# Ordering the square sums of a merge's weights behind the ACT work traced ahead of them

## The chip, the cores and the metric

The kernel runs on one core of one Trainium2 chip. The metric is the device time of one execution, in microseconds (us). TensorE is called PE here, VectorE DVE, ScalarE ACT, GpSimd POOL and SyncE SP; SP issues most of the DMA transfers.

## The reference

One layer of a flow-matching backbone, for 2048 sample tokens and 128 prompt tokens, with a model width of 1024 and three branches of width 512. Cut to what matters here:

```python
proj = einsum('btd,de->bte', xn, w_in)      # xn: RMSNorm with adaLN
o_a = rmsnorm(delta_bidir(q, k, v, g, beta, s0_f, s0_b)) * silu(z_a)
o_b = chunk_sgu(u_b, v_b, sgu_norm_g, w_spatial, b_spatial) * silu(z_b)
o_c = fourier_mix(x_c, grid) * silu(z_c)
br = stack([o_a, o_b, o_c], axis=2)
pb = einsum('btnw,nwd->btnd', br, w_branch)
gt = sigmoid(gates.reshape(B, T, 3, 1024))  # gates: 3072 columns of proj
merged = einsum('btnd,btnd->btd', gt, pb)
y = rmsnorm(h + gate * einsum('btd,de->bte', merged, w_out), final_g)
```

The delta rule of branch A is a scan over chunks of tokens, forward and backward, and each step needs the state that the last step left. All data are float32.

## The kernel before

**Numbers.** A float32 product is made from float16 parts: each operand is scaled by a power of two and split into a high part and a rest, and three matmuls (high by high, high by rest, rest by high) sum up in PSUM. `gemm_T` does that for one weight block of 128 output columns and one token tile: 24 matmuls where the sum runs over 1024, 12 where it runs over 512.

**Weights.** `wlist` holds 84 blocks of weights in the order of their use: 4 for the gate of branch A, 32 for the projections of the branches, then 48 for the merges, a gate block (128 columns of w_in, 1024 by 128) and a branch block (128 columns of w_branch, 512 by 128) in turn. A block is read into a tile `wst` by SP (`read_w`, L195; two buffers) and made ready by the generator `converting`, in three steps:

1. ACT squares the block and sums the squares into `ss` (L209; the squares themselves go into the `lo` tile and are scratch), and DVE rounds the sum to bfloat16 (L175).
2. A small matmul with ones adds up over the partitions, and DVE works out the power-of-two scale and its inverse (L183 to L187, L220).
3. ACT writes the high part `hi` (L222) and DVE the rest `lo` (L223). After that the `wst` buffer is free.

`weight_step` makes one step each time `pace.tick` is called, which is once a token tile; `getw(n, ahead)` hands out the next n blocks, completes them where they aren't ready, and lets `ahead` more be begun. `wnext[0]` counts the blocks handed out.

**Merges.** `merge` runs three times: for branch 1, then 2, then 0. Each time it goes over 8 blocks of 128 output columns, and in each block over five token tiles (four of 512 and one of 128; the first two merges begin with tokens 0 to 1023, the third with the rest). For a tile it traces the gate product (24 matmuls), ACT's sigmoid of it (`sg`, L1385), the branch product (12 matmuls), one DVE pass that multiplies the two (L1391 in the first merge, L1394 in the others), a POOL addition to the running sum `mrow` (L1395), and `pace.tick`. The conversion of a next gate block is begun at the first tick of a block, and that of a next branch block at the fourth. In the third merge each block begins with the conversion of a block of w_out as well (`out_w`, by `load_w`), which goes through the same `converting`.

**The delta scan beside it.** The scan of branch A is a generator that `pace` advances while the projections and the first two merges are traced: some of its steps come out after every second k step of a `gemm_T`. On ACT its work is many small passes: splits into high part and rest (L907), the scaled output (L917, L1051), copies of small blocks (L860 to L894). The scan has ended before the third merge begins.

**What sets the order.** The program is traced in the order of the code; each engine's queue is then ordered by a scheduler at compile time, with its own times for every instruction and transfer: an instruction may go ahead of others that were traced before it when, by these times, its inputs are there and its engine is free. `tc.high_priority()` (around the sigmoid and the scales) ranks work ahead. On the chip every engine takes its queue in order: an instruction that waits holds up all that stand behind it.

Of the kernel before, what the change touches and what calls it, by code (L numbers as in the profile page):

```python
# [14 lines left out]
AF = mybir.ActivationFunctionType  # L15
# [96 lines left out]
def hybrid_flow_kernel(ctx: ExitStack, tc: tile.TileContext, x_prompt, x_sample, state_delta, c, c_ctx, ln_g, w_ada,  # L112
                       b_ada, w_in, conv_w, a_log, dt_bias, o_norm_g, sgu_norm_g, w_spatial, b_spatial, w_branch,
                       w_out, final_g, consts, y_prompt, y_sample, new_state, dbg=None):
    nc = tc.nc
    V, A, G, PE, SY = nc.vector, nc.scalar, nc.gpsimd, nc.tensor, nc.sync
# [9 lines left out]
    def sb(pl, shape, tag, dt=F32, bufs=None):  # L126
        kw = {} if bufs is None else {"bufs": bufs}
        return pl.tile(list(shape), dt, tag=tag, name=nm(tag), **kw)
# [31 lines left out]
    def mm(out, l, r, start=True, stop=True):  # L160
        PE.matmul(out, l, r, start=start, stop=stop)  # L161

    def mm3(out, l, r):
# [2 lines left out]
        mm(out, l[0], r[1], False, False)  # L166
        mm(out, l[1], r[0], False, True)

    def rsqrt(out, ss, mul, w):
        V.tensor_scalar(out, ss, mul, EPS, ALU.mult, ALU.add)  # L170
        G.tensor_tensor(out, out, mhalf.to_broadcast([P, w]), ALU.pow)  # L171

    def widened(ss, pl, tag):
        sb16 = sb(pl, [P, 1], tag + "b", BF16)
        V.tensor_copy(sb16, ss)  # L175
        return sb16

    def scales(ss, pl, tag, sb16=None):

        ps = bank(ps_x, [P, 1])  # L180
        mm(ps, ones16, widened(ss, pl, tag) if sb16 is None else sb16)
        t = sb(pl, [P, 4], tag)
        V.tensor_copy(t[:, 0:1], ps)  # L183
        h = t[:, 3:4].bitcast(I32)
        V.tensor_scalar(h, t[:, 0:1].bitcast(I32), 24, None, ALU.logical_shift_right)
        V.tensor_scalar(t[:, 1:2].bitcast(I32), h, -8388608.0, 204.0 * 8388608, ALU.mult, ALU.add)
        V.tensor_scalar(t[:, 2:3].bitcast(I32), h, 8388608.0, 50.0 * 8388608, ALU.mult, ALU.add)  # L187
        return t[:, 1:2], t[:, 2:3]
# [9 lines left out]
    def converting(w, st, nkt, cols=P, hi=None, lo=None, tag="w", bufs=5):  # L198

        wpool = bwp[0] if tag == "b" else wp  # L200
        if tag == "z":
            hi, lo = [sb(p0p, [P, nkt, cols], n_, F16, bufs=4) for n_ in ("zhi", "zlo")]
        if tag == "v":
            hi, lo = [t[:, vfilled[0]] for t in v4]
            vfilled[0] += 1
        w.hi = sb(wpool, [P, nkt, cols], tag + "hi", F16, bufs=bufs) if hi is None else hi
        w.lo = sb(wpool, [P, nkt, cols], tag + "lo", F16, bufs=bufs) if lo is None else lo
        ss = sb(wp, [P, 1], "wss", bufs=4)
        A.activation(w.lo, st, AF.Square, accum_out=ss)  # L209
        yield  # L210
        sb16 = widened(ss, wp, "wsc")
        if wnext[0] < 11:
            yield
        if wnext[0] < 16:
            s, inv = scales(None, wp, "wsc", sb16)
        else:
            with tc.high_priority():
                s, inv = scales(None, wp, "wsc", sb16)
        w.inv = sb(wp, [P, 1], "winv", bufs=10)
        V.tensor_mul(w.inv, inv, isx)  # L220
        yield
        A.activation(w.hi, st, AF.Copy, scale=s)  # L222
        V.scalar_tensor_tensor(w.lo, st, s, w.hi, ALU.mult, ALU.subtract)  # L223

    def convert(st, nkt, *args, **kw):
        w = _W()
        for _ in converting(w, st, nkt, *args, **kw):
            pass
        return w
# [22 lines left out]
        return xs_[t0:t0 + n, :] if t0 < NS else xp_[t0 - NS:t0 - NS + n, :]  # L252

    wlist = []
    for c0 in [C_ZA + g * P for g in range(4)]:
        wlist.append((w_in_[:, c0:c0 + P], KT, "z", 4))
    for c0 in ([C_QKV + i * P for i in range(12)] + [C_V + g * P for g in range(4)]
# [8 lines left out]
    wdone, wnext, wread, wlate, bwp, wsteps = [], [0], [], [0], [], []  # L266
# [6 lines left out]
    def begin():  # L273

        i = len(wdone)
        if i >= goal[0] or (wlist[i][2] == "b" and not bwp):
            return False
        if len(wread) == i:
            read_next()
        wdone.append(_W())  # L280
        wsteps.append(converting(wdone[i], wread[i], wlist[i][1], tag=wlist[i][2], bufs=wlist[i][3]))
        return True
# [15 lines left out]
    def getw(n=1, ahead=0):  # L298
        i = wnext[0]
        wnext[0] += n  # L300
        fetch(i + n)
        while len(wdone) - len(wsteps) < i + n:
            weight_step()
        fetch(i + n + ahead)
        r = wdone[i:i + n]
        return r[0] if n == 1 else r
# [89 lines left out]
    for blk in range(8):  # L396
# [4 lines left out]
        for k0 in range(0, KT, 4):  # L401
            st = sb(p0p, [P, 4, 256], "ast", bufs=8)
# [39 lines left out]
    for ti, (t0, tn) in enumerate(TBS):  # L442
# [7 lines left out]
        for j in range(nt):  # L450
            A.activation(jk, xt[:, j, :], AF.Square, accum_out=xss[:, j:j + 1])
        rs = sb(p0p, [P, nt], "rs")
        rsqrt(rs, xss, 1.0 / D, nt)
        for j in range(nt):
            V.tensor_scalar(xt[:, j, :], xt[:, j, :], rs[:, j:j + 1], None, ALU.mult)
# [166 lines left out]
    for ct in range(12):  # L622
        w = getw(1, 2 if ct < 6 else min(4, 15 - ct))
# [418 lines left out]
    def finish(t, o):  # L1042
        of = sb(dq, [P, WB], "of")
        SY.dma_start(of, ofD[t])
        G.tensor_tensor(o, o, of, ALU.add)
        ss = sb(dq, [P, H], "oss")
        for h in range(H):
            A.activation(of[:, hs(h)], o[:, hs(h)], AF.Square, accum_out=ss[:, h:h + 1])
        rsqrt(ss, ss, 1.0 / P, H)
        for h in range(H):  # L1050
            A.activation(o[:, hs(h)], o[:, hs(h)], AF.Copy, scale=ss[:, h:h + 1])  # L1051
        yield 1
        ps = bank(ps_out, [P, WB])
        for h in range(H):
            PE.transpose(ps[:, hs(h)], o[:, hs(h)], ident)  # L1055
        SY.dma_start(h3(of), szD[:, :, t * P:(t + 1) * P].rearrange("h p t -> p h t"))
        V.scalar_tensor_tensor(o, ps, ong, of, ALU.mult, ALU.mult)
        A.activation(of, o, AF.Square, accum_out=oss[0][:, t:t + 1])
        SY.dma_start(obD[0][:, :, t * P:(t + 1) * P].rearrange("h p t -> p h t"), h3(o))
# [111 lines left out]
    for t in range(NCH):  # L1171
        ps = bank(ps_mm, [P, 4, P])
        ts = slice(t * P, (t + 1) * P)
        for k in range(KT):
            mm(ps, xh[:, k, ts], v4[0][:, :, k, :], k == 0, False)
            mm(ps, xh[:, k, ts], v4[1][:, :, k, :], False, False)
            mm(ps, xl[:, k, ts], v4[0][:, :, k, :], False, k == KT - 1)
        vn = sb(ep, [P, WB], "sg", bufs=4).rearrange("p (i c) -> p i c", i=4)
        with tc.high_priority():
            V.tensor_tensor(vn, ps, vinv.rearrange("p (i o) -> p i o", o=1).to_broadcast([P, 4, P]), ALU.mult)  # L1180
        sq = sb(ep, [P, WB], "st", bufs=3)
        ss = sb(bp, [P, 1], "vss", bufs=3)
        A.activation(sq, vn.rearrange("p i c -> p (i c)"), AF.Square, accum_out=ss)
        rsqrt(ss, ss, 1.0 / WB, 1)
        if vprev is not None:
            spatial(*vprev)
        if len(vout) > 2:
            vstore()
        V.tensor_scalar(vn, vn, ss, None, ALU.mult)
        vprev = (t, vn)  # L1190
        if t == 8:
            cfill = fourier_consts()
        if t >= 8:
            next(cfill, 0)
        pace.tick(5.2)
# [9 lines left out]
    for g in range(4):  # L1205
# [5 lines left out]
        for ti, (t0, tn) in enumerate(TBS):  # L1211
            st = vrow[:, t0:t0 + tn]
# [349 lines left out]
```

## Time and profile before

| | |
|---|---|
| Median of 3 runs | 2200.02 us (2197.28 to 2202.29) |
| The profiled execution's own time | 2200.34 us |
| Its span, first to last instruction | 2198.2 us |
| Granted PE clock, mean | 0.993 |
| PE busy | 2125.9 us, 97% of the span |
| ACT busy | 1014.4 us, 46% |
| First merge, about | 1050 to 1415 us |
| Second merge, about | 1415 to 1745 us |
| Third merge, about | 1745 to 2020 us |

In the lines of the profile, L161 is line 161 of the kernel; most matmuls have that line, because one helper issues them. `wlo<-wst` is an instruction that reads the tile wst and writes wlo (gate weights); `blo` is the branch weights' tile, `wolo` that of w_out. A group line gives a count (x6), the shortest, median and longest duration in ns, and the first and last start in us. A line in order of time gives the start and the duration in us, and in square brackets how long the engine stood idle before it and what ended the wait. A matmul's duration there is its passage through the array; the next one starts before it has ended.

### The profile page before, as it was taken

What the parts mean: (1) busy time and instruction counts of PE and PEld (TensorE: products, weight loads), DVE (VectorE), ACT (ScalarE), POOL (GpSimd) and SP (SyncE); (2) the same over time, 40 slices, a digit from 0 to 9 for tenths busy, and PEclk for the clock granted to TensorE, in tenths of its full rate; (3) what the DMA queues carried; (4) which work ended last, traced back from release to release, by engine and by line L of the source; (5) the groups of instructions that cost most, each with busy time, mean ns of one, the idle gap of its engine ahead of it and who ended that gap; (6) DMA issues with size and microseconds to landing.
All of it is one profiled execution on the core that took longest, in us unless ns stands there. A gap on an engine that the chain in (4) does not pass through costs nothing. (4 is left out here: it accounts for less than half of the span.)

```text
span 2198.2 us, 42667 instructions
## 1 busy us (share of the span) xinstructions
PE 2125.9 (97%) x16234; PEld 1213.1 (55%) x16234; DVE 1311.2 (60%) x3140; ACT 1014.4 (46%) x2345; POOL 707.5 (32%) x862
## 2 busy tenths in 40 slices
PE   7999999999999999899899999999999999999998
PEld 3565444455555587777555555555654444444443
DVE  5746745469979698466665555765674544223454
ACT  3644644345466474355544445655553422222332
POOL 1421433223333322432322223344532221222543
PEclk9999999999999999999999999999999999999999
DMA  8324733167777662444655556776664544324542
GB/s 280 141 87 149 260 117 110 61 203 231 241 229 239 198 192 83 126 130 137 203 172 162 164 164 185 240 212 209 200 198 151 168 125 133 118 78 123 174 148 103
DMA packets 304568, 365.09 MB, mean 166 GB/s; under 512 B 39426, under 2 KB 215787, under 8 KB 302315
## 3 DMA queue, kind: packets, MB, share of 16 engines
q1 hardware_dynamic: 289226, 302.19, 45.6%
q0 software_dynamic: 12688, 51.27, 6.4%
q10 hardware_dynamic: 2448, 8.91, 1.0%
q8 instruction: 127, 2.08, 0.4%
q14 instruction: 79, 0.64, 0.1%
HBM read 234.67 MB, written 127.62 MB: 165 GB/s over the span
## 5 line engine op out<-in xcount | busy, mean ns | idle before, releaser
L161 PE MATMUL b<-xh,whi 128*128 128x512 f16 (+1 forms) x1920 | 652.8, 349 | 0.4 <-DVE mrow L1391 0.4
L161 PE MATMUL b<-xl,whi 128*128 128x512 f16 (+1 forms) x1920 | 652.9, 348 | 0.0
L161 PE MATMUL b<-xh,wlo 128*128 128x512 f16 (+1 forms) x1920 | 651.9, 348 | 0.5 <-DVE wlo L223 0.5
L161 PEld LDWEIGHTS <-whi 128*128 128x128 f16 x3904 | 358.8, 98 | 330.0 <-issue 9.4
L161 PEld LDWEIGHTS <-wlo 128*128 128x128 f16 x1952 | 191.7, 98 | 180.8 <-issue 5.0
L161 PE MATMUL b<-big,bhi 128*128 128x512 f16 (+1 forms) x960 | 250.6, 347 | 2.4 <-ACT big L1355 1.9
L1395 POOL TENSOR_TENSOR mrow<-mrow,sg 128x512 f32<-128x512 f32 (+1 forms) x80 | 91.8, 1148 | 293.9 <-DVE sg L1394 225.7
L161 PE MATMUL b<-big,blo 128*128 128x512 f16 (+1 forms) x480 | 162.9, 347 | 0.0
L1385 ACT ACTIVATE sg<-b,winv 128x512 f32<-128x512 f32 (+1 forms) x120 | 74.1, 618 | 174.5 <-PE b L161 173.7
L644 POOL TENSOR_TENSOR cy<-cy,raw 128x545 f32<-128x545 f32 (+1 forms) x48 | 74.9, 1586 | 184.2 <-ACT raw L643 184.2
L161 PEld LDWEIGHTS <-xh 128*128 128x128 f16 x1496 | 117.0, 98 | 28.1
L1394 DVE SCALAR_TENSOR_TENSOR sg<-b,binv,sg 128x512 f32<-128x512 f32 (+1 forms) x80 | 53.4, 667 | 126.1 <-PE b L161 119.3
L161 PEld LDWEIGHTS <-bhi 128*128 128x128 f16 x960 | 86.5, 98 | 73.6 <-issue 2.1
L175 DVE CAST wscb<-wss 128x1 bf16<-128x1 f32 x93 | 14.3, 154 | 148.5 <-ACT wlo L209 67.3
L864 POOL COPY T<-ES 32x256 f16<-32x256 f16 x68 | 30.5, 449 | 202.3 <-DMA ES<-ei 167.1
L161 PE MATMUL b<-whi,xh 128*128 128x128 f16 x544 | 92.9, 219 | 0.0
L161 PE MATMUL b<-wlo,xh 128*128 128x128 f16 x544 | 92.9, 219 | 0.0
L161 PE MATMUL b<-whi,xl 128*128 128x128 f16 x544 | 92.9, 219 | 0.0
L161 PE MATMUL b<-wohi,mh 128*128 128x512 f16 x240 | 90.9, 379 | 1.4 <-ACT mh L1462 1.4
L161 PE MATMUL b<-wohi,ml 128*128 128x512 f16 x240 | 90.8, 379 | 0.3 <-DVE mscb L175 0.3
L161 PE MATMUL b<-wolo,mh 128*128 128x512 f16 x240 | 90.9, 379 | 0.0
L209 ACT ACTIVATE wlo<-wst 128x1024 f16<-128x1024 f32 x52 | 55.0, 1057 | 77.5 <-DMA wst<-in_w_in_dram 74.1
(456 smaller groups left out, 4285.4 us busy)
## 6 DMA issues: line engine op xcount, KB each, us to landing
wst<-in_w_in_dram SPq DMA_DIRECT2D x60, 512.0 KB, 4.9
qkv<-cy POOLq DMA_DIRECT2D x12, 1089.0 KB, 5.4
st<-br SPq DMA_DIRECT2D x48, 256.0 KB, 4.6
mrow<-mrg SPq DMA_DIRECT2D x18, 512.0 KB, 3.6
mrow<-mrg SPq DMA_DIRECT2D x16, 576.0 KB
mrg<-mrow POOLq DMA_DIRECT2D x16, 576.0 KB, 3.6
dc<-dec SPq DMA_DIRECT2D x17, 512.0 KB, 4.7
kq<-qkv SPq DMA_DIRECT2D x34, 256.0 KB, 4.6
```

The lines of the kernel that those rows point to most:

```text
L161: PE.matmul(out, l, r, start=start, stop=stop)
L175: V.tensor_copy(sb16, ss)
L209: A.activation(w.lo, st, AF.Square, accum_out=ss)
L644: G.tensor_tensor(y[:, c0:c1], y[:, c0:c1], raw[:, 1 + c0:1 + c1], ALU.mult)
L864: G.tensor_copy(T16[rows(a0, b), :, :, b], ES[0:32, :, 2 * a0 + b, :, wT])
L1385: A.activation(sg, ps, AF.Sigmoid, scale=gw.inv)
L1394: V.scalar_tensor_tensor(sg, ps, binv[:, 1:2], sg, ALU.mult, ALU.mult)
L1395: G.tensor_tensor(mr, mr, sg, ALU.add)
```

## The change

A helper, `pinned`, takes an instruction and looks back through the list of traced instructions for the last six of the same engine; it adds an ordering edge from each of them to the instruction. The edges are of the kind without a semaphore: the scheduler may not put the instruction ahead of those six, and nothing else is asked for.

`converting` calls it for the square sum of a block, as long as `wnext[0]` is at least 38 and below 80. The first merge's opening fetch sets it to 38; each block of a merge adds 2. So the condition holds through the first two merges (16 blocks) and the first five blocks of the third, for gate, branch and w_out weights alike.

```diff
+    def pinned(made, n=6):
+
+        ins = made.ins
+        before = (i for i in reversed(nc.cur_bb.bb.instructions) if i is not ins and i.engine == ins.engine)
+        for _, i in zip(range(n), before):
+            tc.add_manual_dep(ins, i.name, mybir.DependencyInfo(mybir.DependencyClass.NoSync, mybir.DependencyReason.DATA),
+                              reason="pinned")
+        return made
+
...
-        A.activation(w.lo, st, AF.Square, accum_out=ss)
+        sq = A.activation(w.lo, st, AF.Square, accum_out=ss)
+        if MERGES[0] <= wnext[0] < MERGES[1]:
+            pinned(sq)
         yield
...
     wlist = []
+    MERGES = (38, 80)
```

## Prediction

> **What bounds the kernel now.** I read the page first, then busy time by stretch, then TensorE's waits inside the merges, then the order of time on ACT and PE around one of them. A change under 0.2% (4.4 us of 2200) can't be told from none; I count it as "same".
>
> ```profile
> span 2198.2 us, 42667 instructions
> PE 2125.9 (97%) x16234; PEld 1213.1 (55%) x16234; DVE 1311.2 (60%) x3140; ACT 1014.4 (46%) x2345; POOL 707.5 (32%) x862
> ```
>
> ```profile
> 1060.00:1082.00 22.00, 18.00 (x117) 9.69 (x117) 14.30 (x39) 14.95 (x33) 4.22 (x9) 0.77 0.81 253
> 1082.00:1400.00 318.00, 311.59 (x2769) 184.14 (x2768) 185.50 (x489) 153.60 (x367) 83.91 (x128) 1.00 0.59 178
> 1400.00:1720.00 320.00, 313.68 (x2645) 182.72 (x2644) 194.87 (x517) 166.38 (x461) 135.63 (x165) 1.00 0.64 196
> 1720.00:1932.00 212.00, 212.00 (x1183) 102.93 (x1182) 89.67 (x243) 67.95 (x109) 42.70 (x45) 1.00 0.42 131
> ```
>
> The columns are stretch, length, then busy us of PE, weight load, DVE, ACT and POOL, granted clock, DMA share, GB/s. The four rows are the start of the first merge, the rest of it, most of the second, and the part of the third that the change touches. PE is the bound: idle 4.0 us in the first row, 6.4 and 6.3 us in the next two, 0.0 in the last. A change that only orders ACT can win what is idle here and no more, and in the third merge it can only lose.
>
> What PE waited for between 1082 and 1720 us (total us, times, longest):
>
> ```profile
> PE b L1055 <- ACT o L1051: 3.1, 4, 1.1
> PE b L161 <- ACT S L907: 2.8, 4, 1.1
> PE b L161 <- DVE R L880: 1.8, 1, 1.8
> PE b L161 <- ACT Q L862: 1.8, 1, 1.8
> PE b L161 <- DVE S L908: 1.5, 3, 0.7
> PE b L161 <- ACT v L907: 1.0, 2, 0.7
> PE b L161 <- DVE mrow L1391: 0.4, 1, 0.4
> PE b L161 <- DVE v L908: 0.3, 1, 0.3
> ```
>
> That is 12.7 us, nearly all on operands of the delta scan that ACT or DVE made late. Why late shows in the order of time; two fences, ACT and then PE, from one place:
>
> ```profile
> 1249.99 0.69 ACT L1385 ACTIVATE sg<-b,winv 128x512 f32<-128x512 f32 x1 [1.21 <-PE b L161]
> 1254.84 1.06 ACT L209 ACTIVATE wlo<-wst 128x1024 f16<-128x1024 f32 x1 [4.16 <-DMA wst<-in_w_in_dram]
> 1256.40 0.62 ACT L907 ACTIVATE S<-S 128x512 f16<-128x512 f32 x1
> ```
>
> ```profile
> 1253.05 0.38 PE L161 MATMUL b<-xh,whi 128*128 128x512 f16 x1
> 1253.26 0.38 PE L161 MATMUL b<-xl,whi 128*128 128x512 f16 x1
> 1253.48 0.38 PE L161 MATMUL b<-xh,wlo 128*128 128x512 f16 x1
> 1257.08 0.22 PE L161 MATMUL b<-S,sk 128*128 128x128 f16 x1 [0.93 <-ACT S L907]
> ```
>
> A weight square (L209) stood at the head of ACT for 4.16 us until its weights had landed; the split of the state S queued behind it, and PE lost 0.93 us for want of S. The three matmuls above it start 0.21 to 0.22 us apart with no wait: that is PE at its pace, so each such loss adds to the time. I went through the other waits of the table the same way: the twelve put down to S, Q and o (L907, L908, L862, L1051) each come at most 12 us behind a square that stood waiting; the ones on R, v and mrow don't. How much the squares of that stretch waited (us, times):
>
> ```profile
>   DMA wst<-in_w_in_dram: 40.3, 14
>   DMA wst<-in_w_branch_dram: 17.1, 7
> ```
>
> **The change part by part.** *The helper* adds ordering edges between instructions of one engine. ACT runs in order anyway, so no instruction, semaphore or DMA is added: 42667 instructions stay. What moves is the place of squares in ACT's queue, and with it the rest of the schedule that is worked out from it.
>
> *Which squares.* The condition holds from the first merge's opening fetch to the fifth block of the third merge: 33 squares traced in the first two merges, 10 in the third, and 5 of w_out there: 48.
>
> *How far.* Rows of squares and sigmoids up to 1255 us:
>
> ```profile
> L209 ACT ACTIVATE blo<-wst x6: 617/626/633, 1047.4 to 1233.2; 128x512 f16<-128x512 f32 x6
> L209 ACT ACTIVATE wlo<-wst x6: 1047/1056/1057, 1048.1 to 1254.8; 128x1024 f16<-128x1024 f32 x6
> L1385 ACT ACTIVATE sg<-b,winv x22: 350/685/688, 1055.4 to 1250.0; 128x512 f32<-128x512 f32 x18, 128x128 f32<-128x128 f32 x4
> ```
>
> 22 sigmoids are four blocks of five tiles and two tiles of block 4. The sixth gate square (the first one of this window is block 1's) is block 6's; the program traces it after the first tile of block 5. So it ran four tiles before its place, as soon as its read had been planned to land. Likewise the sixth branch square, block 5's, ran at 1233.2, ahead of block 4; it is traced after block 4's fourth tile. The pin takes both back behind the sigmoid of the tile they are traced after and behind the scan's ACT work in between. The read is not moved by an edge, so it has some three tiles to land, and the waits of 40.3 and 17.1 us go. Each read needs one of two wst buffers, which the last pass (L223) frees; squares four tiles later free it later, the next read stands longer at the head of SP, and the scan's reads queue behind it. No row shows that; its bounds are 0 and the late-weights case below, and I take 0, because a read still comes a tile or more ahead of its square.
>
> *What that returns.* At most 3.1+2.8+1.8+1.5 = 9.2 us. S and Q (6.1) I take whole: the S row starts as soon as the square leaves ACT. Of the 3.1 on o I take half, 1.5, because o's scale also comes through POOL. Term: -7.6, bounds -9.2 and 0.
>
> *What it costs: the branch weights.* The gate square still has four tiles until use. The branch square has one narrow tile and the next block's gate product. ACT, then PE, around the fourth tile of a block:
>
> ```profile
> 1231.71 0.63 ACT L907 ACTIVATE S<-S 128x512 f16<-128x512 f32 x1 [0.41 <-DVE S L1018]
> ```
>
> ```profile
> 1230.79 0.38 PE L161 MATMUL b<-big,blo 128*128 128x512 f16 x1
> 1240.43 0.59 PE L161 MATMUL b<-big,bhi 128*128 128x512 f16 x2
> 1240.87 0.38 PE L161 MATMUL b<-big,blo 128*128 128x512 f16 x1
> ```
>
> and the way from a square to finished weights, where nothing else holds it:
>
> ```profile
> 1849.19 0.63 ACT L209 ACTIVATE blo<-wst 128x512 f16<-128x512 f32 x1 [5.26 <-DMA wst<-in_w_branch_dram]
> 1852.50 0.17 PE L161 MATMUL b<-wscb,ones 128*128 128x1 bf16 x1
> 1853.78 0.72 ACT L222 ACTIVATE bhi<-wst,wsc 128x512 f16<-128x512 f32 x1 [3.14 <-DVE wsc L186]
> 1854.98 0.75 DVE L223 SCALAR_TENSOR_TENSOR blo<-wst,wsc,bhi 128x512 f16<-128x512 f32 x1
> ```
>
> The chain takes 1854.98 + 0.75 - 1849.19 = 6.54 us. The fourth tile's last branch matmul is the one at 1230.79; the scan's ACT work traced up to there ends, I take it, with the S split, at 1231.71 + 0.63 = 1232.34. So blo is ready at 1238.88 and read at 1240.87: slack 2.0 us, where before there were four tiles more. Cover is the narrow tile, the gate product and the scan's matmuls; without it PE waits 1 us for each us. 15 such blocks in the first two merges: I take 0.1 us each, +1.5; bounds 0 (PE waits for no branch weight now, so there is nothing to win) and +15 (1 us each). In the third merge a full tile follows (36 matmuls of 0.216 us, 7.8 us) and the gate product (24, 5.2 us): 13 against 6.5, so 0. Its w_out squares feed the output stage only: 0.
>
> *The start of the first merge.* The first branch square has no lead; ACT, POOL, PE, and PE's waits from 1045 to 1082 us:
>
> ```profile
> 1047.45 0.63 ACT L209 ACTIVATE blo<-wst 128x512 f16<-128x512 f32 x1
> ```
>
> ```profile
> 1056.89 1.68 POOL L1137 TENSOR_TENSOR st<-sg,yT 128x512 f32<-128x512 f32 x2
> ```
>
> ```profile
> 1065.04 0.61 PE L161 MATMUL b<-big,bhi 128*128 128x512 f16 x1
> ```
>
> ```profile
> PE b L161 <- ACT S L907: 2.5, 1, 2.5
> PE b L161 <- ACT big L1355: 1.9, 2, 1.6
> ```
>
> The pin puts that square behind the squares (L1138) of the Fourier products that POOL makes until 1056.89 + 1.68 = 1058.57. With two of those passes, by 1060.5 as an estimate, it is ready at 1067.0, 2 us after its use at 1065.04. Against it stand the two waits, 4.4 us, both right behind waiting squares. I take -1, bounds +6 (the weights 6 us late) and -4.4; and the clock: 0.77 over 22 us is 5.1 us lost, which could go with the gap.
>
> By the Trainium skill (TensorE: Matmul & The Clock Gate, the HAM clock gate) the clock halves after an idle window of about 3.4 us; by that no wait here would do it, the longest being 2.5 us, and nothing could be won from it. The 0.77 says that it did fall; I put 0 in the sum and 5.1 us at the low end.
>
> *Sum.* -7.6 + 1.5 - 1 = -7.1 us. The profiled execution took 2200.34 us (span 2198.2, 2.1 around it), 0.3 above the median of 2200.0; so 2193.2 by it and 2192.9 by the median: 2193.
>
> **The rivals.** *Late branch weights, slower, 0.20.* If the pinned square leaves ACT more than 2.0 us after the S split, PE waits for blo in every block. The scan's ACT work itself waits for reads and for DVE, and the square now stands behind it. For: the slack is a third of the chain. Against: the schedule is worked out with the chain in it and can put other matmuls ahead. It decides from 7.6/15 = 0.5 us lateness a block; at 1 us it gives +15 - 7.6 - 1 = +6.4: 2206.
>
> *Another wait ends just behind, same, 0.20.* The 3.5 us on R, v and mrow show that the scan has waits of its own. If half of the 9.2 us is taken over by these, -4.6 + 1.5: 2197.
>
> *PE has room anyway, or the squares don't move, same, 0.04.* If idle PE time were made up later, nothing would change: 2200. The matmuls 0.22 us apart speak against it; the counts of squares speak against no move.
>
> The Trainium skill (Perfetto Trace Analysis, Identifying the Most-Contended Engine) says that matmul busy time is a bad measure and weight-load share a good one. By it PE would be 57% full in the second merge (182.72 of 320) and this rival would hold; the spacing of the matmuls decides against it.
>
> **How the numbers follow.** Forecast 0.56, rivals 0.20, 0.20, 0.04. Low end: all 9.2 and 4.4 us and some of the clock, -15: 2185. High end: the slower rival, 2206. Faster by over 0.2% 0.56, same 0.24, slower 0.20. The forecast's own range is 2185 to 2195.6.
>
> **What would show it.** Right: in the profile after, squares of the first two merges with almost no wait on wst; PE's waits on S, Q and o between 1082 and 1720 us down from 9.2 to about 2 us; gate squares just behind a block's first sigmoid, branch squares behind the fourth. Wrong: PE waiting for blo, bhi or the scale (L223, L222); or squares as early as before; or the 9.2 us gone with the time not down, when the start of the first merge (idle, clock) or work behind 1720 us has taken it.

## The result and the profile after

| | before | after |
|---|---|---|
| Median, same chip, 6 runs each | 2198.65 us (2194.03 to 2202.29) | 2222.64 us (2219.3 to 2226.19) |
| Ratio, 95% interval | | 1.011 [1.0097, 1.0122] |
| The profiled execution | 2200.34 us | 2219.3 us |
| Granted PE clock, mean | 0.993 | 0.987 |

The change makes the kernel 24 us slower. The forecast was 7 us faster, with a range that ended at 2206. Three executions among the runs below took 2752 to 3107 us at a granted clock of 0.67 to 0.75; the medians count them, the ratios do not.

The page of after, its span and its first part:

```profile
span 2217.5 us, 42667 instructions
PE 2133.2 (96%) x16234; PEld 1218.6 (55%) x16234; DVE 1319.1 (59%) x3140; ACT 1015.2 (46%) x2345; POOL 706.6 (32%) x862
```

The instructions are the same, as the helper promises. To find the 19 us between the two profiled executions I cut each at its own merges: from the first sigmoid of a merge to the first of the next, the third to its last sigmoid. Busy time by stretch (columns as in the prediction: length, then PE, weight load, DVE, ACT, POOL, granted clock, DMA share, GB/s), before and then after:

```profile
1055.40:1418.70 363.30, 348.72 (x3115) 207.01 (x3112) 219.22 (x582) 184.33 (x442) 98.50 (x150) 0.99 0.62 187
1418.70:1750.10 331.40, 327.20 (x2633) 186.16 (x2630) 196.57 (x512) 169.56 (x453) 136.18 (x162) 1.00 0.62 192
1750.10:2011.40 261.30, 261.30 (x1441) 126.71 (x1439) 86.25 (x244) 66.45 (x109) 52.81 (x55) 1.00 0.36 112
```

```profile
1051.70:1410.20 358.50, 346.81 (x3086) 204.84 (x3083) 218.85 (x571) 181.39 (x427) 99.91 (x149) 0.98 0.61 187
1410.20:1769.70 359.50, 339.56 (x2669) 194.52 (x2668) 200.72 (x514) 170.47 (x467) 138.92 (x163) 0.97 0.60 178
1769.70:2030.30 260.60, 260.05 (x1437) 126.28 (x1436) 88.07 (x258) 70.77 (x114) 52.64 (x55) 1.00 0.36 115
```

The first merge begins 3.7 us earlier and is 4.8 us shorter; the third is as long as before. The second merge is 28.1 us longer, and that is the whole loss. PE idles there 359.50 - 339.56 = 19.9 us instead of 4.2, so 15.7 us more. Its busy time is 339.56 - 327.20 = 12.4 us more. Together that is the 28.1. Part of the longer busy time is the clock, 0.97 instead of 1.00.

The squares between 1082 and 1720 us, after, as a group with what it waited for and who waited for it:

```profile
L218 ACT ACTIVATE blo<-wst x14: 612/614/647, 1099.8 to 1693.7; 128x512 f16<-128x512 f32 x14
...
L218 ACT ACTIVATE wlo<-wst x14: 1039/1044/1072, 1113.8 to 1696.0; 128x1024 f16<-128x1024 f32 x14
...
its engine sat idle before it (us, times) until:
who waited for it (us, times):
  DVE wscb L184: 19.9, 17
```

Under "sat idle before it" stands nothing. The 57.4 us for which squares waited on their reads are gone, as foretold. But what PE waited for in the same stretch (total us, times, longest) is not:

```profile
PE b L161 <- ACT u L919: 3.9, 3, 2.9
PE b L161 <- ACT Q L874: 3.2, 2, 2.6
PE b L161 <- DVE wscb L184: 3.1, 2, 2.9
PE b L161 <- DVE o L1069: 2.4, 2, 1.2
PE b L161 <- DVE u L920: 2.0, 3, 0.8
PE b L161 <- DVE S L920: 1.7, 2, 1.3
PE b L161 <- ACT bhi L233: 1.7, 3, 0.9
PE b L161 <- DMA ES<-ei: 1.3, 1, 1.3
PE b L161 <- ACT S L919: 1.1, 2, 0.9
PE b L161 <- ACT o L929: 1.0, 1, 1.0
...
```

These ten rows alone are 21.4 us, where the whole table of before had 12.7. Q, o and S have 9.4 us in it, no less than the 9.2 of before. Only wscb and bhi (4.8 us) name branch weights or their scale; the rest names the scan, and read alone it would send one to look for a slow scan. The order of time shows otherwise. ACT of after around the first sigmoid of block 12, the fifth of the second merge (L1397 is the sigmoid, L218 the square, L233 the high part; L1060 and L1063 are scan passes that finish an output chunk):

```profile
1596.44 0.69 ACT L1397 ACTIVATE sg<-b,winv 128x512 f32<-128x512 f32 x1 [0.45 <-PE b L161]
...
1598.24 0.31 ACT L1060 ACTIVATE of<-o 128x128 f32<-128x128 f32 x1 [0.86 <-POOL o L1057]
...
1600.05 0.37 ACT L874 ACTIVATE Q<-b 32x256 f16<-32x256 f32 x1
1600.45 0.63 ACT L919 ACTIVATE S<-S 128x512 f16<-128x512 f32 x1
1600.98 1.26 ACT L1063 ACTIVATE o<-o,oss 128x128 f32<-128x128 f32 x4
1602.15 0.61 ACT L218 ACTIVATE blo<-wst 128x512 f16<-128x512 f32 x1
...
1607.93 0.72 ACT L233 ACTIVATE bhi<-wst,wsc 128x512 f16<-128x512 f32 x1
```

The square of the weights that block 12 multiplies by starts 5.7 us behind block 12's own first sigmoid. In front of it stand the scan's closing passes, the first of which itself waits for POOL. The high part follows 5.8 us later. PE in the same time:

```profile
1596.02 0.38 PE L161 MATMUL b<-xh,wlo 128*128 128x512 f16 x1
...
1597.14 0.77 PE L161 MATMUL b<-u,kn 128*128 128x128 f16 x11 [0.48 <-DVE u L920]
1600.47 0.27 PE L161 MATMUL b<-Q,ES 128*128 128x32 f16 x4 [2.56 <-ACT Q L874]
...
1602.64 1.33 PE L161 MATMUL b<-S,sk 128*128 128x128 f16 x11 [0.46 <-DVE S L920]
1604.20 0.21 PE L161 MATMUL b<-wscb,ones 128*128 128x1 bf16 x1
...
1609.02 1.04 PE L161 MATMUL b<-big,bhi 128*128 128x512 f16 x2
```

The gate product ends at 1596.0, and the branch product, which needs bhi, begins at 1609.0. For 13 us PE starts no product, only the scan's small matmuls, and these depend on each other through ACT and DVE. So the waits carry the scan's names, but what is missing is the branch weights. Before, the same block:

```profile
1586.52 0.72 ACT L222 ACTIVATE bhi<-wst,wsc 128x512 f16<-128x512 f32 x1
...
1595.21 0.69 ACT L1385 ACTIVATE sg<-b,winv 128x512 f32<-128x512 f32 x1
```

There bhi was begun 8.7 us ahead of that sigmoid.

Other late blocks have other scan passes directly in front of the square. At the second and third block of the second merge it is the scaled output (L929), which had waited for a read and for PE:

```profile
1459.18 1.14 ACT L929 ACTIVATE o<-b,eg 128x128 f32<-128x128 f32 x4 [3.37 <-DMA br<-o]
1460.20 0.65 ACT L218 ACTIVATE blo<-wst 128x512 f16<-128x512 f32 x1
...
1504.40 1.14 ACT L929 ACTIVATE o<-b,eg 128x128 f32<-128x128 f32 x4 [3.07 <-PE b L161]
```

Of the seven late blocks (leads under 6.5 us in the table below) three have the scaled output last in front, three a closing pass (L1063, L1070) and one the split of u (L919).

The clock completes the picture; busy time by stretch of after at two late blocks, the first and the fifth of the second merge:

```profile
1406.00:1412.50 6.50, 4.41 (x37) 2.63 (x36) 4.24 (x10) 4.14 (x12) 1.04 (x1) 1.00 0.90 280
1412.50:1422.70 10.20, 7.67 (x61) 5.12 (x61) 7.56 (x25) 6.17 (x21) 6.26 (x9) 0.50 0.62 194
1592.00:1600.20 8.20, 5.43 (x50) 3.19 (x48) 3.43 (x11) 3.51 (x13) 3.45 (x5) 1.00 0.49 154
1600.20:1610.40 10.20, 8.01 (x77) 6.15 (x77) 7.74 (x21) 6.15 (x17) 3.71 (x5) 0.50 0.95 257
```

At both, PE is busy for some two thirds of 6 to 8 us, and then the granted clock is 0.50 for 10.2 us. With a third, shorter stretch (1695.8 to 1699.2 us, 3.00 us busy) PE is at 0.50 for 23.8 us of that merge and busy for 18.7 of them. At full clock this work would take half as long, so the clock's part of the 28.1 us is about 9.3, as an estimate.

### The profile page after: what moved, and what is told of

It is laid out like the page before. It is cut to its first block, busy times and chain, and to the rows that moved or that the text cites. A ratio compares the mean times of both kernels' runs of the same rounds, so it can differ in the third digit from the quotient of the medians.

```text
span 2217.5 us, 42667 instructions
## 1 busy us (share of the span) xinstructions
PE 2133.2 (96%) x16234; PEld 1218.6 (55%) x16234; DVE 1319.1 (59%) x3140; ACT 1015.2 (46%) x2345; POOL 706.6 (32%) x862
## 4 chain that ended last, share of the span: by engine, by line
PE 48%; DMA 6%; DVE 5%; ACT 2%; POOL 1%; issue 1%; SPq 0%; DVEq 0%; POOLq 0%; ACTq 0%
PE b L161 48%; DMA st<-br 2%; DVE XB L807 1%; DMA ES<-ei 0%; DVE E L808 0%; DVE big L1368 0%; DVE sg L398 0%; DMA wst<-in_w_ada_dram 0%; DMA skn<-kv 0%; DMA ei<-XB 0%; DMA br<-o 0%; ACT big L1367 0%; DMA mrow<-mrg 0%; DMA mrg<-mrow 0%; PE b L1067 0%
## 5 line engine op out<-in xcount | busy, mean ns | idle before, releaser
L161 PEld LDWEIGHTS <-whi 128*128 128x128 f16 x3904 | 360.7, 98 | 337.1 <-issue 12.5
L1397 ACT ACTIVATE sg<-b,winv 128x512 f32<-128x512 f32 (+1 forms) x120 | 74.4, 620 | 189.3 <-PE b L161 188.6
L161 PEld LDWEIGHTS <-xh 128*128 128x128 f16 x1496 | 117.0, 98 | 28.1
L656 POOL TENSOR_TENSOR cy<-cy,raw 128x545 f32<-128x545 f32 (+1 forms) x48 | 69.8, 1483 | 184.4 <-ACT raw L655 184.4
L234 DVE SCALAR_TENSOR_TENSOR wlo<-wst,wsc,whi 128x1024 f16<-128x1024 f32 x52 | 72.1, 1392 | 32.2 <-ACT whi L233 32.1
```

Of the source, the lines that this page charges most:

```text
L656: G.tensor_tensor(y[:, c0:c1], y[:, c0:c1], raw[:, 1 + c0:1 + c1], ALU.mult)
L1397: A.activation(sg, ps, AF.Sigmoid, scale=gw.inv)
```

## The experiments

Three theories were put to the test. **A, late branch weights:** a branch square behind six ACT instructions comes too late for its block. **B, gate squares:** gate squares that run later free the `wst` buffers later, and so delay the reads. **C, any order:** the schedule before is fitted so closely that each reordering costs. All ratios are against the kernel before on the same chip (its medians there were 2196.87 to 2197.39 us).

**Only the gate squares, only the branch squares.** One condition each:

```diff
-        if MERGES[0] <= wnext[0] < MERGES[1]:
+        if MERGES[0] <= wnext[0] < MERGES[1] and tag == "w" and bufs == 4:     # e1_gate
+        if MERGES[0] <= wnext[0] < MERGES[1] and tag == "b":                   # e2_branch
```

> Only the gate weights' squares are ordered behind the six; branch and w_out squares are free as before. Theory A (late branch weights: the branch square, pinned, stands behind the scan's passes and comes too late for its own block): the gain of the first merge stays and the loss of the second goes, 5 to 10 us under the kernel before, 2190. Theory B (the gate squares hold the two wst buffers for four tiles and the reads behind them come late): most of the loss stays, 15 us or more over before, 2214. Theory C (any new order of the scan against the products costs, whichever square moves): somewhere from -5 to +25 us, without relation to the parts.

> Only the branch weights' squares are ordered behind the six. Theory A: the loss of the second merge comes back, with little of the gain: +20 to +35 us over before, 2220 to 2234, with TensorE waiting for the scale and the high part of branch weights. Theory B: about as before, 2199 within 5 us. Theory C: no relation to the whole change.

The gate edges alone: 2195.99 us, 0.9991 [0.998, 1.0002]. The branch edges alone: 2224.85 us, 1.0118 [1.0093, 1.0143], as much as the whole change. B and C fall. Of A the loss is confirmed; the gain that A expected of the gate run (2190) is not there. It wins 1.4 us, an amount that its interval does not tell from zero, of the 7.6 that were forecast. Its squares hardly waited any more (between 1082 and 1720 us: what its group waited for), and yet PE's waits in its first merge add up to 14.1 us, where before they were 14.3. The three largest:

```profile
  DMA wst<-in_w_branch_dram: 5.3, 2
```

```profile
PE b L161 <- DMA ES<-ei: 4.6, 1, 4.6
PE b L161 <- ACT u L919: 3.0, 1, 3.0
PE b L161 <- ACT v L919: 1.3, 1, 1.3
...
```

A read of the scan and two splits took the place of S and Q; that merge is 363.3 us long, to the tenth what it was before.

**One merge alone.** `MERGES = (38, 54)` pins in the first merge, `MERGES = (54, 70)` in the second.

> The edges only while blocks 38 to 53 are handed out, that is in the first merge, all kinds of squares. In the changed kernel the first merge ended some 8 us earlier than before and the second took some 28 us longer. Theory A: the first merge's scan steps are forward ones without the passes that finish a chunk, so the branch squares come in time there: 5 to 9 us under before, 2190 to 2194. Theory B and C: the gain of the first merge is not tied to it, 2199 to 2210.

> The edges only while blocks 54 to 69 are handed out, that is in the second merge. Theory A: the loss sits here, +20 to +30 us over before, 2219 to 2229. Theory B: the same loss, but with waits at the scan's reads rather than for branch weights. Theory C: the loss differs by more than 10 us from the 28 us that the second merge lost in the whole change.

The first alone: 2204.37 us, 1.0032 [1.0014, 1.0049], a miss: it is slower, not faster, and the number by itself lies in the range that was named for B and C. The second alone: 2210.53 us, 1.0063 [1.0042, 1.0083], half of what was expected. The profiles point to the reason. In the first run the first merge stays short (358.5 us), but the last square that is still pinned there is the branch square of the second merge's first block. It starts 2.3 us behind that block's first sigmoid, the block takes 50.7 us instead of 44.8, and the second merge 340.5. In the second run just that block is in time, and its merge takes 342.2 us. So the loss belongs to single blocks of the second merge, not to the merge as a whole.

**Other orders for the branch squares.** The first run puts the branch square behind the last traced sigmoid alone, and leaves the gate and w_out squares behind six; the very first branch square is free. The second leaves the six but traces the branch square two tiles earlier in its block. The third pins each square behind one instruction.

```diff
+    lastsg = []                                                   # e5_sigmoid
...
-            pinned(sq)
+            if tag == "b":
+                for made in lastsg[-1:]:
+                    tc.add_manual_dep(sq.ins, made.ins.name, ...)
+            else:
+                pinned(sq)
...
-                        A.activation(sg, ps, AF.Sigmoid, scale=gw.inv)
+                        lastsg.append(A.activation(sg, ps, AF.Sigmoid, scale=gw.inv))
```

```diff
+            tile_no = 0
...
                     pace.tick(tn * MT)
+                    tile_no += 1                                  # e6_early
+                    if tile_no < 3:
+                        weight_step()
```

```diff
-    def pinned(made, n=6):
+    def pinned(made, n=1):                                        # e7_one
```

> As the change, but a branch weight's square stands only behind the sigmoid of the tile at whose tick it is traced, not behind the scan's passes traced after that; the first one of all is free. In the planned order it then comes right behind the fourth sigmoid of a block, where the change had it behind the fifth or the next block's first in the second merge. Theory A (the square comes too late for its own block, because it stands behind passes that finish a chunk): most of the 26 us that the branch edges cost goes, 2195 to 2205. Theory C (any later place of the branch square costs as much): 2215 or more.

> As the change, with one more conversion step in each of a block's first two tiles, so that the branch square is traced after the second tile instead of the fourth; it is still ordered behind six. Theory A: the lateness is gone with two tiles of lead, 2190 to 2200. Theory C: the edges still reorder everything, 2210 or more.

> As the change, behind one instruction instead of six. Theory A: the last one traced is a pass of the scan in nearly every case, so the square comes hardly sooner: 2212 to 2228. If the number six mattered by itself: 2205 or less.

Behind the sigmoid: 2194.89 us, 0.9994 [0.998, 1.0008], the loss is gone. ACT of this run around the same block 12:

```profile
1574.31 0.69 ACT L1403 ACTIVATE sg<-b,winv 128x512 f32<-128x512 f32 x1 [0.51 <-PE b L161]
1574.90 0.62 ACT L218 ACTIVATE blo<-wst 128x512 f16<-128x512 f32 x1
...
1578.47 0.72 ACT L238 ACTIVATE bhi<-wst,wsc 128x512 f16<-128x512 f32 x1
...
1587.37 0.68 ACT L1403 ACTIVATE sg<-b,winv 128x512 f32<-128x512 f32 x1
1587.95 0.30 ACT L1066 ACTIVATE of<-o 128x128 f32<-128x128 f32 x1
```

The square directly follows the sigmoid of its tile, and the scan's closing passes (L1066 here) come behind it. It leads the block's first sigmoid by 12.5 us. That is the cleanest test of the mechanism: the gate squares stay behind six as in the change, the branch squares are still held to the tile they are traced in, and the scan's passes that were traced after that sigmoid need no longer be ahead of them. Which of these passes matters most was not tried.

Two tiles earlier: 2204.01 us, 1.0031 [1.002, 1.0043], above the 2190 to 2200 that A expected. The second merge is back at 332.1 us, but the kernel isn't. The added step also runs in the third merge, which no scan work fills. Waits of PE there, and the stretch with it:

```profile
PE b L161 <- DVE sg L1407: 3.7, 2, 3.4
PE b L161 <- DVE wscb L184: 1.1, 1, 1.1
```

```profile
1748.30:2013.50 265.20, 260.42 (x1437) 126.39 (x1436) 87.29 (x257) 69.01 (x113) 53.82 (x55) 1.00 0.36 112
```

The third merge takes 265.2 us against 261.3 before, with 4.8 us of idle PE. These 3.9 us are part of the 6.8 that the medians differ by; the rest isn't placed. Behind one instruction: 2219.24 us, 1.0095 [1.0078, 1.0111]. Three blocks of that run are late as well, so the number six is not the point.

**Can the gain be kept?** Three runs, and one for a single block:

```diff
+        if MERGES[0] <= wnext[0] < MERGES[1] and tag == "w" and bufs == 4:     # e8_gate2: MERGES = (54, 70); e9_gate40: (40, 70)
+        if MERGES[0] <= wnext[0] < MERGES[1] and (wnext[0] < 52 or tag == "w" and bufs == 4):     # e10_both: MERGES = (38, 70)
+        if wnext[0] == 52 and tag == "b":                                      # e11_single
```

> Only gate squares, and only in the second merge, where their edges left that merge 4 us shorter while the first merge kept its length. Theory A: 2 to 6 us under before, 2192 to 2196. If the 4 us were chance of the arrangement: 2196 to 2202.

> Only gate squares, from the second block of the first merge to the end of the second merge; the opening of the first merge is as before. With gate squares alone the first merge kept its length although the squares' waits were gone from it, and its opening had a new wait of 4.6 us for a read of the scan and 10.2 us at half clock. If the gain of the first merge was lost at its opening, it shows now: first merge 3 to 6 us shorter than before, the second 4, 2189 to 2193. If other waits of the scan take the place of the squares' all along: the first merge within 2 us of before, 2193 to 2197.

> All squares in the first merge up to its seventh block, gate squares alone after that to the end of the second merge. If branch squares cost only where they come late for their block (the last block of the first merge and the second merge), the first merge keeps the 5 us that the whole change won there and the second wins its 4: 2187 to 2192. If any branch edge costs: 2197 or more.

> One edge set alone: the square of one branch weight block, the second merge's first, which is traced in the last block of the first merge; all others are free as before. In the planned order it stands behind the first sigmoid of its own block. Theory A (each branch square that comes late for its own block costs by itself, by waits and by the half clock that follows): in the changed kernel that place has 4.6 us of waits and 10.2 us at half clock, so 4 to 10 us over before, 2201 to 2207. If the loss needed many late squares or comes from the rest of the rearranged schedule: within 3 us of before.

Gate squares of the second merge alone: 2194.56 us, 0.9975 [0.9963, 0.9988]. Gate squares from the first merge's second block on: 2193.7 us, 0.9983 [0.9971, 0.9994]. Both are below both kernels and the lowest of the eleven; against before it is 2.6 and 3.2 us by the medians, 5.5 and 3.7 by the ratios. The first merge of the second run takes 362.5 us, so it met the expectation that other waits of the scan take the place of the squares'. The third run was to join the short first merge to these and missed: 2197.02 us, 0.9999 [0.9987, 1.0011]; its first merge takes 362.9 us again. It came out where its expectation puts "if any branch edge costs"; against that stands the run behind the sigmoid, which orders the branch squares of all three merges and has no loss. The last was meant as a dose, one late block. Its square led by 8.7 us and wasn't late, and there was no loss (so no run shows one late block by itself): 2196.24 us, 0.9995 [0.9985, 1.0005]. It has a use as a yardstick. Its squares waited as before:

```profile
  DMA wst<-in_w_in_dram: 42.6, 13
  DMA wst<-in_w_branch_dram: 13.2, 6
```

and its second merge took 328.5 us all the same, against 331.4 before and 327.2 in the run with all gate squares pinned. So of the 4.2 us that the gate run seems to win in the second merge, 2.9 come in a kernel whose squares still wait. What removing the waits returns is not told apart from that.

**All runs in one table.** The lead is the start of a block's first sigmoid less the start of that block's branch square. Finished weights need 6.5 us from the square (block 12 of after: 1607.93 + 0.72 - 1602.15 = 6.50). The shortage adds up, over the eight blocks of the second merge, what each lead lacks of 6.5; the leads are worked out from the traces.

| kernel | leads, second merge, us | shortage | second merge, against 331.4 |
|---|---|---|---|
| before | 31.7 to 50.7 | 0 | |
| e1_gate | 21.3 to 41.2 | 0 | -4.2 |
| e8_gate2 | 20.9 to 50.5 | 0 | -3.7 |
| e9_gate40 | 21.4 to 39.8 | 0 | -3.5 |
| e11_single | 8.7 to 46.0 | 0 | -2.9 |
| e5_sigmoid | 9.2 to 16.6 | 0 | -1.8 |
| e10_both | 13.2 to 36.6 | 0 | -1.2 |
| e6_early | 7.4 to 31.3 | 0 | +0.7 |
| e3_first | -2.3, then 30.4 to 49.2 | 8.8 | +9.1 |
| e4_second | 49.5 8.0 10.9 5.0 -5.0 3.2 -2.4 9.2 | 25.2 | +10.8 |
| e7_one | 7.5 7.0 9.6 -3.6 -2.5 1.8 11.3 9.2 | 23.8 | +23.2 |
| after | -2.2 3.2 0.6 4.9 -5.7 3.3 -2.4 9.2 | 43.8 | +28.1 |
| e2_branch | -5.7 2.3 2.1 -1.3 -3.0 3.0 -2.4 9.3 | 50.5 | +31.8 |

In the second merge, where no block lacks lead the loss is 0.7 us at most, whatever else moved; where blocks lack lead it is 0.4 to 1.0 us for each us of shortage. In the first merge of after the leads of the second to eighth block are 6.8 to 11.5 us: short, but enough. Its first block has a lead of -4.3 us and takes only 0.7 us longer than before (56.2 against 55.5), so the relation is not one for every place.

## Why the prediction was wrong

- **What moves, and the squares' waits: right.** 42667 instructions stay, the squares no longer wait on reads, and no row of PE's waits names a read of weights.
- **The branch weights, "+1.5", and the failed step: the lead.** The step took the slack from one place, the fourth tile of a block in the first merge, and from the line "the scan's ACT work traced up to there ends, I take it, with the S split". There it held: in after the square of that block starts at 1227.91, right behind an S split, and leads by 8.5 us, where the step's 1232.34 gives 8.4 against the old sigmoid at 1240.76. In the second merge the scan's traced work at that point also holds the scaled output and the passes that finish an output chunk, which wait for reads, PE, POOL and DVE; the square stands behind all of it and starts up to 5.7 us behind the sigmoid by which its weights are wanted. So the slack of 2.0 us is missing at seven blocks, and the term of +1.5 measures +28.1 by the second merge and about +26 by the ratio of the branch run. Leads differ from block to block by 15 us (after: -5.7 to 9.2), so one place could not stand for fifteen. The bound of +15 was too low as well.
- **The slower rival was the right mechanism at a quarter of its price.** "PE waits for blo in every block" at 1 us each gave +6.4. Two things were missing from the price. A late block left PE the scan alone, so the loss is the time between products, not only the wait that carries the weights' name. And the thinned work is followed by the halved clock, about 9.3 of the 28.1 us by the estimate above. "The schedule ... can put other matmuls ahead" did not hold: at block 12 no product stood between 1596.0 and 1609.0.
- **The gain, "-7.6": not there either.** The gate run shows -1.4 us (0.9991 [0.998, 1.0002]). In it the waits on S, Q and o between 1082 and 1720 us do fall, from 9.2 to 2.7 us, near the 2 that the prediction named as a sign; but all of PE's waits there fall only from 12.7 to 9.0, since u and v are waited for instead. That is the second rival. And the single-block run, whose squares wait as before, has 4.3 us on S, Q and o, so a good part of the fall needs no pin. That a wait ends last is not yet that the time after it is free: the scan is a chain, and its next operand has its own history.
- **The start of the first merge, "-1", and the third merge, "0": about right.** The first branch square does leave late (4.3 us behind the first sigmoid, where before it led by 8.0), and PE waits 0.9 us for its scale (wscb) and 2.1 us for its high part (bhi), which the prediction put 2 us late. Against that the 4.4 us of waits on S and big are gone. The first block takes 56.2 us instead of 55.5: +0.7 against -1, what is left of two larger amounts. The merge's 3.7 us earlier begin is no gain of the change: in the single-block run, in which nothing ahead of the merges is pinned, it begins at 1052.1, 3.3 us earlier as well.
- **What stays open.** The first merge is 4.6 to 4.8 us shorter in after, in the branch run and in the first-merge run, but not in the other runs that pin squares there (361.7 to 363.3 us); no run tells why. Where the gain of the two lowest runs comes from isn't placed. The shares of waits and of the clock were read from the traces and not tried one by one; which scan pass in front of the squares costs most wasn't tried either, and why the scheduler has no other product for PE at the late blocks wasn't tried.

## What to carry to other kernels

An ordering edge passes on what the instructions ahead of it depend on: the pinned one cannot start before they do. Look at what those instructions wait for at each place of the loop, not at one. For work that feeds the bound engine, write down the lead of each block against the length of its chain: leads that lacked 1.6 to 12.2 us at seven blocks cost 28 us here, three times the 9.2 that the removed waits could have returned. And where waits are named on a side chain, ask first which main work should have stood in the queue at that time.

## What the runs showed of the hardware

The clock fell without a long pause. At the first block of the second merge the fall to 0.50 is at 1412.5 us, and PE's longest wait around it was 1.0 us (on o, L929); at block 12 it is at 1600.2 us, inside a wait of 2.56 us. In the last 3.40 us ahead of the fall PE was busy for 1.31 us and for 0.77 us, in small matmuls with waits between them. The Trainium skill (TensorE: Matmul & The Clock Gate, the HAM clock gate) names an idle window of about 3.4 us as what halves the clock. If that is taken as one unbroken wait, these rows disagree: a stretch of that length with PE busy for a quarter to two fifths of it was enough. The prediction, which put 0 on the clock in its sum, took it so, and had its own row against that reading in the 0.77 of the first merge's start.
